# Where the last two expert groups of a mixture-of-experts layer are summed into the output

## The chip, the core and the metric

One core of a Trainium2 chip runs the whole layer in one launch. The metric is device time in microseconds (us) of one execution. TensorE (PE) multiplies, VectorE (DVE) and ScalarE (ACT) move and transform, GpSimd (POOL) helps, and the SyncE queue (SP) issues nearly all transfers.

## The reference

A decoder layer on 256 tokens of width 1024, float32: norm, one input projection, two kinds of attention, an output projection with a residual, and then a mixture of experts. The change touches only the end of the last part:

```python
g = jnp.argmax(g_logits, axis=-1)                 # 1 of 4 groups for each token
top_v, top_e = lax.top_k(e_logits, 2)             # 2 of the 8 experts in it
weight = p_group * jax.nn.softmax(top_v, axis=-1)
def run(args):                                    # for each expert e on its tokens
    xc = t[toks]
    hid = jax.nn.silu(xc @ w_gate[e]) * (xc @ w_up[e])
    return hid @ w_down[e]
y = jnp.zeros((N, D), t.dtype).at[slot_tok].add((out * slot_w[:, None]).astype(t.dtype))
x = x + hier_moe(...)                             # the residual
```

There are 32 experts; gate and up are 1024 x 256, down is 256 x 1024, so each matrix is 1 MB and the experts' weights are 96 MB.

## The kernel before

The kernel goes through the experts in order, as steps e = 0 to 31, and works on them in eight groups of four (G = 4, not the reference's groups). Each expert has 32 slots for tokens (CAP), so that a group fills 128 partitions.

- `prep(g)`, in the last step of the group before, builds with `places` a 0/1 matrix of slots (tiles Pm and Ps) and gathers the group's tokens by 32 PE passes (L615) into the tile xe.
- In step e, `gate` and `up` multiply the tokens of expert e by its two matrices (16 PE passes each, since a float32 product of the program is two passes in the trace; L658); `folded` transposes the result of expert e-1 (L675) and makes hT on DVE and ACT; `down` multiplies hT of expert e-2 by its down matrix (L693) and moves the product out of PSUM into the group's tile oG (L707 on ACT and L709 on DVE, four pieces).
- `weighted(st)` scales the slot matrix by the tokens' weights W, transposes it on PE (L642) and keeps it as pT. `combine(st)`, two steps into the next group, adds pT times oG of the whole group into the output sums y, which stay in four PSUM banks (L728, full 128 rows).
- The last group goes another way: `weighted_last` makes four repeated matrices, one for each expert (L628 on DVE, L630 on PE, L631 on ACT), into a tile oL; `moved` takes a down product out of PSUM in two pieces (L712, L713); and `spread` adds one expert's product into y with four 32-row tiles of PE (L718). `residual` adds the residual, which POOL copied to the tile res (L906), by a product with the identity (L733).
- `last` does the down product of expert 31, and the copies of y to res (L750, L752) and from there to the output (L753), in two halves.

PE keeps its program order (`pe`). Weights come through a ring of 16 one-megabyte tiles and seven more slots (`fill`, `unit`); SP issues each load as soon as the tile's last reader is done and an earlier load has landed. After step 28's down product stands `overflow`, a branch on whether an expert has more than 32 tokens; all engines pass it, and the body was not run here.

Of the kernel before, what the change touches and what calls it, by code (L numbers as in the profile page):

```python
# [9 lines left out]
F32 = mybir.dt.float32  # L10
# [4 lines left out]
AF = mybir.ActivationFunctionType  # L15
# [5 lines left out]
P = 128  # L21
# [30 lines left out]
def hybrid_layer_kernel(ctx: ExitStack, tc: tile.TileContext, x, xt, w_in, w_out, w_gate, w_up, w_down, smalls, relb, out):  # L52
# [534 lines left out]
    u = 16  # L587
    G = 4
    x2n = x2q.rearrange("t c k p -> t c p k")
    CROSS = [(j, c) for c in range(NC) for j in range(4)]  # L590
    g2p = A_COLS["g2p"][0]

    def places(g, c):
# [23 lines left out]
            gathered(st, q4, pg, 0, P)  # L617
        return st

    def weighted_last(st):  # L620
        t = pools["late"].tile([P, 2048], F32, name="oL", tag="late")
        st["o"], st["pT"] = t[:, :D].rearrange("p (i n) -> p i n", i=G), t[:, D:].rearrange("p (i t) -> p i t", i=G)
        for i in range(G):
            pt = ps.tile([P, 512], F32, name="ptr", tag="tr")
            for c in range(NC):
                q = st["P"][c][1].rearrange("p (j s) -> p j s", j=G)
                e = st["g"] * G + i
                nc.vector.tensor_scalar(q, st["P"][c][0][:, i : i + 1, :].broadcast_to([P, G, CAP]),  # L628
                                        W[:, c, e : e + 1], None, op0=ALU.mult)
                pe(nc.tensor.transpose(pt[:, c * P : (c + 1) * P], q.rearrange("p j s -> p (j s)"), ident))  # L630
            nc.scalar.activation(st["pT"][:, i, :], pt[:, :S], AF.Copy)  # L631

    def weighted(st):
        g = st["g"]
        if g == E // G - 1:
            return weighted_last(st)
# [59 lines left out]
    def down(e, st, hT, low):  # L696
        i = e % G
        dv = unit(place[e][2], low).rearrange("p (c n) -> p c n", c=2)
        pd = ps.tile([P, 512], F32, name="pd", tag="tr")
        down_product(hT, dv, pd, range(2), range(4))  # L700
        if st["g"] == E // G - 1:
            moved(st, i, pd, slice(0, P))
            return
        for j in range(4):
            dst = st["o"][i * CAP : (i + 1) * CAP, j * 256 : (j + 1) * 256]
            if j % 2 == 0:
                nc.scalar.activation(dst, pd[j * 32 : (j + 1) * 32, :256], AF.Copy)  # L707
            else:
                nc.vector.tensor_copy(dst, pd[j * 32 : (j + 1) * 32, :256])  # L709

    def moved(st, i, pd, rows):
        nc.scalar.activation(st["o"][rows, i, :P], pd[rows, :P], AF.Copy)  # L712
        nc.vector.tensor_copy(st["o"][rows, i, P:], pd[rows, P:256])  # L713

    def spread(st, i, pairs):
        for j, c in pairs:
            r = slice(j * CAP, (j + 1) * CAP)
            pe(nc.tensor.matmul(y[j][:, c * 256 : c * 256 + 256], st["pT"][r, i, c * P : (c + 1) * P],  # L718
                                st["o"][r, i, :], start=False, stop=i == G - 1 and c == NC - 1, tile_position=(j * CAP, 0)))

    y = []

# [13 lines left out]
    def last(e, st, hT, res):  # L736
        dv = unit(place[e][2]).rearrange("p (c n) -> p c n", c=2)
        pd = ps.tile([P, 512], F32, name="pd", tag="tr")
        down_product(hT, dv, pd, (0,), range(4))
        warmed(2, "pp")  # L740
        for nh in range(2):
            down_product(hT, dv, pd, (1,), (2 * nh, 2 * nh + 1))
            moved(st, G - 1, pd, slice(nh * 64, nh * 64 + 64))
            j0 = 2 * nh
            spread(st, G - 1, [(j, c) for c in range(NC) for j in (j0, j0 + 1)])
            for c, eng in enumerate((nc.scalar, nc.sync)):
                for j in (j0, j0 + 1):
                    dst = res[:, c, j * 256 : (j + 1) * 256]
                    if j == j0:
                        nc.scalar.activation(dst, y[j][:, c * 256 : c * 256 + 256], AF.Copy)  # L750
                    else:
                        nc.vector.tensor_copy(dst, y[j][:, c * 256 : c * 256 + 256])  # L752
# [127 lines left out]
    before, queue = None, []  # L880
    for e in range(1, E):
        g, i = divmod(e, G)
        old, old_t = st, t
        if i == 0:
            before, st = old, nxt
        t = gate(e, st)
        queue.append((e - 1, old, folded(old_t)))
        if i == 2 and g > 0:
            combine(before)
        up(e, st, t)  # L890
        if i == G - 1 and g < E // G - 1:
            nxt = prep(g + 1)
        if i == 2:
            weighted(st)
        if e == E - 1:
            hT = folded(t)
        if e > 1:
            down(*queue.pop(0), place[e][0])
        if e == OVER_E:
            overflow()  # L900
        if e == E - 1:
            rt_ = ring.tile([P, 2048], F32, name="res", tag="ring")
            res = rt_.rearrange("p (c n) -> p c n", c=NC)
# [4 lines left out]
    spread(st, 0, CROSS)  # L908
    spread(st, 1, CROSS)
    down(*queue.pop(0), place[E - 1][0])  # L910
    residual(0, res)
    residual(1, res)
    spread(st, 2, CROSS)
    last(E - 1, st, hT, res)


_OUTS = [((1, 256, 1024), "float32")]
# [71 lines left out]
```

## Time and profile before

| | |
|---|---|
| median of 3 runs | 344.23 us (343.37 to 344.47) |
| the profiled execution's own time | 344.96 us |
| its span | 343.2 us |
| busy PE, DVE, ACT, POOL | 314.5, 194.3, 139.9, 17.3 us |
| transfers | 123.20 MB, mean 359 GB/s |

The span runs from the first to the last recorded event; the execution's own time has 1.76 us more around it. Busy times are sums over stages with different limits, so the prediction reads stretches and single waits. Times such as 322.10 are us from the start of the span.

### The profile page before, as it was taken

The numbers are of one execution on the slowest core, as the hardware profiler recorded it, in microseconds if no ns is written. First come the engines' busy times: TensorE is split into PE (matmuls) and PEld (weight loads), VectorE is DVE, ScalarE is ACT, GpSimd is POOL, SyncE is SP. The second block draws the span as 40 slices with busy tenths as digits, with TensorE's granted clock in tenths as the row PEclk, the third lists the DMA queues.
The fourth block names the chain that finished last, engine by engine and source line by source line (L and its number), as shares of the span: only waits on it lengthen the run. The fifth ranks groups of instructions, "written<-read, shape, count | busy, mean of one in ns | idle before, by whom it ended". The sixth has DMA issues, their size and how long they took to land. (4 is left out here: it accounts for less than half of the span.)

```text
span 343.2 us, 7327 instructions
## 1 busy us (share of the span) xinstructions
PE 314.5 (92%) x2801; PEld 217.4 (63%) x2801; DVE 194.3 (57%) x599; ACT 139.9 (41%) x364; POOL 17.3 (5%) x25
## 2 busy tenths in 40 slices
PE   6999999999999999999999999998489669968893
PEld 2758877788777797576666766566257326625461
DVE  1867858869998658665463654736224522532502
ACT  4876667968886443423232232321112211211302
POOL 1100001000110140000000000000000000040000
PEclk9899999999999999999999999999989978989997
DMA  6999999999635888899999999999999999999903
GB/s 197 403 385 317 389 387 402 413 411 409 209 99 210 319 355 320 303 423 418 416 416 415 415 421 418 413 421 413 416 418 416 418 415 420 416 411 420 362 10 122
DMA packets 29496, 123.20 MB, mean 359 GB/s; under 512 B 2295, under 2 KB 3364, under 8 KB 21268
## 3 DMA queue, kind: packets, MB, share of 16 engines
q1 hardware_dynamic: 28868, 121.17, 89.1%
q0 software_dynamic: 304, 1.02, 1.0%
q8 instruction: 23, 0.38, 0.4%
q10 hardware_dynamic: 288, 0.52, 0.4%
q14 instruction: 13, 0.11, 0.1%
HBM read 121.64 MB, written 1.07 MB: 358 GB/s over the span
## 5 line engine op out<-in xcount | busy, mean ns | idle before, releaser
L658 PE MATMUL pgu<-u,xe 128*32 128x256 f32 x976 | 67.4, 395 | 10.1 <-ACT oG L707 4.8
L254 PE MATMUL pp<-hi,xh 128*128 128x512 f32 (+1 forms) x132 | 53.3, 405 | 2.6 <-ACT hi L243 2.6
L254 PE MATMUL pp<-lo,xh 128*128 128x512 f32 (+1 forms) x132 | 52.1, 399 | 0.3 <-POOL lo L244 0.2
L254 PE MATMUL pp<-hi,xl 128*128 128x512 f32 (+1 forms) x132 | 51.9, 393 | 0.0
L707 ACT ACTIVATE oG<-pd 32x256 f32<-32x256 f32 x56 | 21.0, 374 | 75.0 <-PE pd L693 61.4
L658 PEld LDWEIGHTS pgu<-u,xe 128*32 128x32 f32 x976 | 29.5, 111 | 34.6 <-ACT oG L707 8.6
L244 DVE TENSOR_TENSOR lo<-u,hi 128x512 fp32r<-128x512 f32 x62 | 43.1, 714 | 13.0 <-ACT hi L243 12.7
L243 ACT ACTIVATE hi<-u 128x512 fp32r<-128x512 f32 x64 | 38.9, 626 | 18.3 <-PE pp L254 12.6
L709 DVE COPY oG<-pd 32x256 f32<-32x256 f32 x56 | 23.7, 423 | 38.7 <-ACT oG L707 36.8
L693 PE MATMUL pd<-u,hT 128*32 128x256 f32 x496 | 34.9, 394 | 6.6 <-DMA u<-in_w_down_dram 6.6
L254 PEld LDWEIGHTS pp<-hi,xh 128*128 128x128 f32 x132 | 25.1, 190 | 9.6 <-ACT hi L243 4.0
L254 PEld LDWEIGHTS pp<-lo,xh 128*128 128x128 f32 x132 | 25.3, 192 | 7.4 <-issue 1.0
L254 PEld LDWEIGHTS pp<-hi,xl 128*128 128x128 f32 x132 | 25.2, 191 | 4.6
L670 DVE COPY u<-pgu 128x256 f32<-128x256 f32 x30 | 12.7, 422 | 26.7 <-PE pgu L658 23.6
L615 PEld LDWEIGHTS pg<-Ps,x2q 128*128 128x128 f32 x224 | 25.5, 192 | 2.9 <-DVE gu L678 2.9
L693 PEld LDWEIGHTS pd<-u,hT 128*32 128x32 f32 x496 | 14.5, 112 | 20.0 <-DVE u L670 7.5
L615 PE MATMUL pg<-Ps,x2q 128*128 128x128 f32 x224 | 26.9, 278 | 0.0
L728 PE MATMUL y<-oG,pT 128*128 128x256 f32 x112 | 26.4, 391 | 0.0
L728 PEld LDWEIGHTS y<-oG,pT 128*128 128x128 f32 x112 | 21.8, 200 | 2.8
L678 DVE TENSOR_REDUCE gu<-ptr 128x64 f32<-128x256 f32 x32 | 13.6, 425 | 14.5 <-PE ptr L675 13.8
L675 PEld LDWEIGHTS ptr<-sm,u 128*128 128x128 f32 x120 | 13.4, 147 | 13.1 <-issue 9.9
L675 PE MATMUL ptr<-sm,u 128*128 128x128 f32 x120 | 21.0, 301 | 0.0
(166 smaller groups left out, 342.0 us busy)
## 6 DMA issues: line engine op xcount, KB each, us to landing
u<-in_w_up_dram SPq DMA_DIRECT2D x31, 1024.0 KB, 19.9
u<-in_w_gate_dram SPq DMA_DIRECT2D x30, 1024.0 KB, 19.9
u<-in_w_down_dram SPq DMA_DIRECT2D x30, 1024.0 KB, 19.9
u<-in_w_in_dram SPq DMA_DIRECT2D x11, 1024.0 KB, 12.0
u<-in_w_out_dram SPq DMA_DIRECT2D x4, 1024.0 KB, 14.6
x<-in_w_gate_dram SPq DMA_DIRECT2D x2, 1024.0 KB, 9.0
u<-in_w_in_dram SPq DMA_DIRECT2D x2, 512.0 KB, 6.0
x<-in_x_dram SPq DMA_DIRECT2D x2, 512.0 KB, 10.9
```

What stands on the lines that cost most here:

```text
L243: nc.scalar.activation(hi, raw, AF.Copy)
L244: (nc.gpsimd if u * 4 + k in (0,3,) else nc.vector).tensor_tensor(lo, raw, hi.bitcast(F32), op=ALU.subtract)
L254: yield lambda a=a, w=w, kk=kk, i=i: nc.tensor.matmul(pp, a, w[:, cols], start=first and kk == 0 and i == 0, stop=last and kk == len(hls) ...
L615: pe(nc.tensor.matmul(pg[:, j * P : (j + 1) * P], x2q[:, c, q4 * 4 + j, :], st["P"][c][1], start=c == 0, stop=c == NC - 1))
L658: pe(nc.tensor.matmul(pg[q * CAP : (q + 1) * CAP, :HID], st["xe"][:, k, j0 : j0 + CAP], wv[:, k, :], start=r == 0, stop=r == KC // ROWS_Q ...
L670: nc.vector.tensor_copy(t[:, HID : 2 * HID], pg[:, :HID])
L675: pe(nc.tensor.transpose(pt[:, j * P : (j + 1) * P], t[:, j * P : (j + 1) * P], ident))
L678: nc.vector.tensor_reduce(gu[:, :2], parts[:, :2], axis=AX.X, op=ALU.add)
L693: pe(nc.tensor.matmul(pd[j * 32 : (j + 1) * 32, :256], hT[:, c, :], dv[:, c, j * 256 : (j + 1) * 256], start=c == 0, stop=c == 1, tile_pos ...
L707: nc.scalar.activation(dst, pd[j * 32 : (j + 1) * 32, :256], AF.Copy)
L709: nc.vector.tensor_copy(dst, pd[j * 32 : (j + 1) * 32, :256])
L728: pe(nc.tensor.matmul(y[j][:, c * 256 : c * 256 + 256], st["pT"][:, c * P : (c + 1) * P], st["o"][:, j * 256 : (j + 1) * 256], start=st["g ...
```

## The change

It treats the last two groups (6 and 7, steps 24 to 31; APART = 6) as the last one was treated before. Their four repeated transposes are split off as `repeated` (DVE) and `weighted_last` (PE, ACT), one a step in steps 24 to 27, and two a step in steps 28 and 29. `spread` of expert e stands in the step after its `down`, for all of experts 24 to 28; `combine` of group 6 goes. The residual's first half stands at the end of step 30 and its second ahead of the down product of expert 30. The tiles oL (two of them) and res come from the ring. `last` does the last down product and the last `spread` whole, and then all copies, four on ACT and four on DVE. The core of the diff:

```diff
+    def spare(name):
+        used["ring"].append(len(units))
+        return ring.tile([P, 2048], F32, name=name, tag="ring")
+    def repeated(st, i):
+        e = st["g"] * G + i
+        for c in range(NC):
+            q = st["P"][c][1].rearrange("p (j s) -> p j s", j=G)
+            nc.vector.tensor_scalar(q, st["P"][c][0][:, i : i + 1, :].broadcast_to([P, G, CAP]),
+                                    W[:, c, e : e + 1], None, op0=ALU.mult)
+    def weighted_last(st, i):
+        pt = ps.tile([P, 512], F32, name="ptr", tag="tr")
+        for c in range(NC):
+            pe(nc.tensor.transpose(pt[:, c * P : (c + 1) * P], st["P"][c][1], ident))
+        nc.scalar.activation(st["pT"][:, i, :], pt[:, :S], AF.Copy)
...
-        if st["g"] == E // G - 1:
-            moved(st, i, pd, slice(0, P))
+        if st["g"] >= APART:
+            moved(st, i, pd)
...
+    def last(st, hT, dv, pd, res):
         for nh in range(2):
             down_product(hT, dv, pd, (1,), (2 * nh, 2 * nh + 1))
+        moved(st, G - 1, pd)
+        spread(st, G - 1)
+        for c in range(NC):
+            for j in range(4):
+                dst = res[:, c, j * 256 : (j + 1) * 256]
+                if j < 2:
+                    nc.scalar.activation(dst, y[j][:, c * 256 : c * 256 + 256], AF.Copy)
+                else:
+                    nc.vector.tensor_copy(dst, y[j][:, c * 256 : c * 256 + 256])
+            for nh, eng in enumerate((nc.scalar, nc.sync)):
                 eng.dma_start(out[c * P : (c + 1) * P, nh * 512 : nh * 512 + 512], res[:, c, nh * 512 : nh * 512 + 512])
...
         if i == 0:
             before, st = old, nxt
+            if g >= APART:
+                last_group(st)
         t = gate(e, st)
         queue.append((e - 1, old, folded(old_t)))
-        if i == 2 and g > 0:
+        apart = () if g < APART else (i,) if g == APART else ((0, 1), (2, 3), (), ())[i]
+        if apart:
+            repeated(st, apart[0])
+        if i == 2 and 0 < g <= APART:
             combine(before)
         up(e, st, t)
+        for k, j in enumerate(apart):
+            if k:
+                repeated(st, j)
+            weighted_last(st, j)
         if i == G - 1 and g < E // G - 1:
             nxt = prep(g + 1)
-        if i == 2:
+        if i == 2 and g < APART:
             weighted(st)
+        if done:
+            spread(*done.pop())
...
+            if st2["g"] >= APART:
+                done.append((st2, e2 % G))
...
+        if e == E - 2:
+            residual(0, res)
+    residual(1, res)
     down(*queue.pop(0), place[E - 1][0])
-    residual(0, res)
-    residual(1, res)
-    spread(st, 2, CROSS)
-    last(E - 1, st, hT, res)
+    spread(*done.pop())
+    dv = unit(place[E - 1][2]).rearrange("p (c n) -> p c n", c=2)
+    pd = ps.tile([P, 512], F32, name="pd", tag="tr")
+    down_product(hT, dv, pd, (0,), range(4))
+    spread(st, 2)
+    warmed(2, "pp")
+    last(st, hT, dv, pd, res)
```

PE's order from the up product of expert 30 (weights u_3102) to the down product of expert 30, before. Here u_3177 and u_3278 are the down weights of experts 28 and 29, x_64 and u_3224 the gate and up weights of expert 31, u_3280 the down weights of expert 30:

```order
L658 MATMUL pgu<-u_3102,xe 32x256 x8
L630 MATMUL ptr<-sm,Ps 128x128 x8
L693 MATMUL pd<-u_3177,hT 32x256 x8
L658 MATMUL pgu<-x_64,xe 32x256 x8
L675 MATMUL ptr<-sm,u_3100 128x128 x4
L658 MATMUL pgu<-u_3224,xe 32x256 x8
L675 MATMUL ptr<-sm,x_64 128x128 x4
L693 MATMUL pd<-u_3278,hT 32x256 x8
L718 MATMUL y<-oL 128x256 x16
L693 MATMUL pd<-u_3280,hT 32x256 x8
L733 MATMUL y<-res,sm 128x256 x8
L718 MATMUL y<-oL 128x256 x8
```

The same place of PE now; the weights have other numbers (u_3180, u_3291, u_3293, u_3295), the lines have moved by six:

```order
L664 MATMUL pgu<-u_3102,xe 32x256 x8
L724 MATMUL y<-oL 128x256 x8
L699 MATMUL pd<-u_3180,hT 32x256 x8
L739 MATMUL y<-res,sm 128x256 x4
L664 MATMUL pgu<-x_64,xe 32x256 x8
L681 MATMUL ptr<-sm,u_3100 128x128 x4
L664 MATMUL pgu<-u_3291,xe 32x256 x8
L724 MATMUL y<-oL 128x256 x8
L681 MATMUL ptr<-sm,x_64 128x128 x4
L699 MATMUL pd<-u_3293,hT 32x256 x8
L739 MATMUL y<-res,sm 128x256 x4
L699 MATMUL pd<-u_3295,hT 32x256 x8
```

The eight transposes are gone from here, the spreads of experts 27 and 28 and both halves of the residual have come in ahead of the down product of expert 30, and a spread stands between expert 31's up product and its transposes.

The end of PE's order before, from the first half of the down product of expert 31 (u_3282):

```order
L693 MATMUL pd<-u_3282,hT 32x256 x4
L688 LDWEIGHTS zeros
L688 MATMUL warm<-zeros 128x512
L688 LDWEIGHTS zeros
L688 MATMUL warm<-zeros 128x512
L693 MATMUL pd<-u_3282,hT 32x256 x2
L718 MATMUL y<-oL 128x256 x4
L693 MATMUL pd<-u_3282,hT 32x256 x2
L718 MATMUL y<-oL 128x256 x4
```

And now, from the down product of expert 30:

```order
L699 MATMUL pd<-u_3295,hT 32x256 x8
L724 MATMUL y<-oL 128x256 x8
L699 MATMUL pd<-u_3345,hT 32x256 x4
L724 MATMUL y<-oL 128x256 x8
L694 LDWEIGHTS zeros
L694 MATMUL warm<-zeros 128x512
L694 LDWEIGHTS zeros
L694 MATMUL warm<-zeros 128x512
L699 MATMUL pd<-u_3345,hT 32x256 x4
L724 MATMUL y<-oL 128x256 x8
```

Two half spreads behind two quarter products have become one whole spread behind one half product; ahead of it stand the spreads of experts 29 and 30.

DVE's order in step 27 before, from the copy of the up product of expert 26 (u_2855) on; L599 writes the slot matrices Ps of group 7, u_2934 is expert 27's:

```order
L670 COPY u_2855<-pgu 128x256
L599 TENSOR_SCALAR Ps<-Pm,rstd 128x128 x2
L709 COPY oG<-pd 32x256 x2
L678 TENSOR_REDUCE gu<-ptr 128x64
L680 TENSOR_REDUCE gu<-ptr 128x64
L682 TENSOR_TENSOR hT<-gu 128x64
L670 COPY u_2934<-pgu 128x256
```

And now, with L632 for the repeated matrix of expert 27 and L719 for the new way out of PSUM:

```order
L676 COPY u_2855<-pgu 128x256
L632 TENSOR_SCALAR Ps<-Pm,W 128x128 x2
L597 TENSOR_TENSOR Pm<-R_1577,sm 128x128 x2
L719 COPY oL<-pd 128x128
L684 TENSOR_REDUCE gu<-ptr 128x64
L686 TENSOR_REDUCE gu<-ptr 128x64
L688 TENSOR_TENSOR hT<-gu 128x64
L676 COPY u_2934<-pgu 128x256
L599 TENSOR_SCALAR Ps<-Pm,rstd 128x128 x2
```

The two writes of Ps for group 7 have moved from ahead of step 27's work to behind the copy of expert 27's up product, since the transposes of expert 27 read those tiles till then.

## Rows read from the trace of the kernel before

**Rows 1.** The first line of the page.

```profile
span 343.2 us, 7327 instructions
```

**Rows 2.** Stretches: length, busy PE, PEld, DVE, ACT, POOL, granted clock, DMA share, GB/s.

```profile
280.00:290.00 10.00, 9.45 (x74) 6.11 (x74) 2.64 (x8) 1.77 (x5) 0.00 (x0) 0.75 1.02 416
305.00:310.00 5.00, 4.67 (x48) 1.86 (x38) 1.47 (x4) 0.88 (x3) 3.62 (x4) 0.66 1.02 413
328.00:335.00 7.00, 6.49 (x50) 4.09 (x46) 0.45 (x2) 0.55 (x2) 0.00 (x0) 1.00 0.00 0
```

**Rows 3.** SP's issue of the up weights of expert 31, in the timeline.

```profile
300.77 0.33 SPq L138 DMA_DIRECT2D u<-in_w_up_dram  x1
```

**Rows 4.** The page's list of loads: these, with the median time to landing last.

```profile
u<-in_w_up_dram SPq DMA_DIRECT2D x31, 1024.0 KB, 19.9
```

**Rows 5.** SP's longest wait of 280 to 310 us: total, times, longest.

```profile
SPq L138 <- DMA u<-in_w_gate_dram: 8.4, 4, 2.1
```

**Rows 6.** Timeline, steps 27 to 30: start, length, engine, line, tiles, passes, idle before and releaser.

```profile
292.68 3.84 PE L615 MATMUL pg<-Ps,x2q 128*128 128x128 f32 x32
...
293.15 0.42 DVE L670 COPY u<-pgu 128x256 f32<-128x256 f32 x1
...
300.89 1.07 PE L693 MATMUL pd<-u,hT 128*32 128x256 f32 x16 [0.93 <-DMA u<-in_w_down_dram]
...
303.28 0.43 DVE L709 COPY oG<-pd 32x256 f32<-32x256 f32 x1 [0.44 <-ACT oG L707]
...
304.42 1.07 PE L658 MATMUL pgu<-u,xe 128*32 128x256 f32 x16 [2.46 <-DVEq L758]
...
310.86 1.07 PE L658 MATMUL pgu<-u,xe 128*32 128x256 f32 x16 [1.17 <-DMA u<-in_w_gate_dram]
...
312.36 3.62 PE L728 MATMUL y<-oG,pT 128*128 128x256 f32 x16
...
316.91 0.44 PE L630 MATMUL ptr<-sm,Ps 128*128 128x128 f32 x2
...
319.65 1.07 PE L693 MATMUL pd<-u,hT 128*32 128x256 f32 x16
```

**Rows 7.** Timeline, step 31 to the end, same columns.

```profile
321.10 0.29 DVE L713 COPY oL<-pd 128x128 f32<-128x128 f32 x1 [1.76 <-ACT oL L712]
...
321.52 0.66 PE L675 MATMUL ptr<-sm,u 128*128 128x128 f32 x4
...
322.10 1.07 PE L658 MATMUL pgu<-u,xe 128*32 128x256 f32 x16
...
325.09 2.01 PE L718 MATMUL y<-oL 32*128 32x256 f32 x32
...
327.03 1.07 PE L693 MATMUL pd<-u,hT 128*32 128x256 f32 x16
...
328.03 3.72 PE L733 MATMUL y<-res,sm 128*128 128x256 f32 x16
...
331.68 1.15 PE L718 MATMUL y<-oL 32*128 32x256 f32 x16
...
332.76 0.64 PE L693 MATMUL pd<-u,hT 128*32 128x256 f32 x8
...
333.87 0.62 PE L693 MATMUL pd<-u,hT 128*32 128x256 f32 x4
...
335.18 1.13 PE L718 MATMUL y<-oL 32*128 32x256 f32 x8 [0.69 <-DVE oL L713]
...
337.74 1.13 PE L718 MATMUL y<-oL 32*128 32x256 f32 x8 [0.87 <-DVE oL L713]
...
338.94 0.76 DVE L752 COPY res<-y 128x256 f32<-128x256 f32 x2 [1.26 <-PE y L718]
```

**Rows 8.** Output rate, 330 to 343.2 us in 40 bins of 0.33 us.

```profile
GB/s 0 0 0 0 0 0 0 0 0 0 0 0 0 0 0 0 0 0 0 0 0 0 0 43 385 385 379 360 37 0 0 292 410 360 391 137 0 0 0 0
```

More of the change, by code (lines that the diff above doesn't have):

```diff
@@ L589, in hybrid_layer_kernel @@
     x2n = x2q.rearrange("t c k p -> t c p k")
-    CROSS = [(j, c) for c in range(NC) for j in range(4)]
+    APART = E // G - 2
     g2p = A_COLS["g2p"][0]
@@ L618, in prep, with last_group @@
         return st
-    def weighted_last(st):
-        t = pools["late"].tile([P, 2048], F32, name="oL", tag="late")
-        st["o"], st["pT"] = t[:, :D].rearrange("p (i n) -> p i n", i=G), t[:, D:].rearrange("p (i t) -> p i t", i=G)
[L623 to L631, printed above, removed]
+    def spare(name):
+        used["ring"].append(len(units))
+        return ring.tile([P, 2048], F32, name=name, tag="ring")
+    def last_group(st):
+        t = spare("oL")
+        st["o"], st["pT"] = t[:, :D].rearrange("p (i n) -> p i n", i=G), t[:, D:].rearrange("p (i t) -> p i t", i=G)
+    def repeated(st, i):
[9 more added lines that the diff above has]
+        nc.scalar.activation(st["pT"][:, i, :], pt[:, :S], AF.Copy)
     def weighted(st):
         g = st["g"]
-        if g == E // G - 1:
-            return weighted_last(st)
         pt = ps.tile([P, 512], F32, name="ptr", tag="tr")
@@ L709, in down, with moved, spread @@
                 nc.vector.tensor_copy(dst, pd[j * 32 : (j + 1) * 32, :256])
[L711 to L716, printed above, removed]
+    def moved(st, i, pd):
+        nc.scalar.activation(st["o"][:, i, :P], pd[:, :P], AF.Copy)
+        nc.vector.tensor_copy(st["o"][:, i, P:], pd[:, P:256])
+    def spread(st, i):
+        for c, j in [(c, j) for c in range(NC) for j in range(4)]:
             r = slice(j * CAP, (j + 1) * CAP)
             pe(nc.tensor.matmul(y[j][:, c * 256 : c * 256 + 256], st["pT"][r, i, c * P : (c + 1) * P],
-                                st["o"][r, i, :], start=False, stop=i == G - 1 and c == NC - 1, tile_position=(j * CAP, 0)))
+                                st["o"][r, i, :], start=False, stop=st["g"] == E // G - 1 and i == G - 1 and c == NC - 1, tile_position=(j * CAP, 0)))
     y = []
@@ L734, in residual @@
                                 start=False, stop=False))
[L736 to L740, printed above, removed]
+    def last(st, hT, dv, pd, res):
         for nh in range(2):
             down_product(hT, dv, pd, (1,), (2 * nh, 2 * nh + 1))
[L743 to L752, printed above, removed]
+        moved(st, G - 1, pd)
[8 more added lines that the diff above has]
+            for nh, eng in enumerate((nc.scalar, nc.sync)):
                 eng.dma_start(out[c * P : (c + 1) * P, nh * 512 : nh * 512 + 512], res[:, c, nh * 512 : nh * 512 + 512])
@@ L879, in hybrid_layer_kernel @@
         nc.vector.tensor_copy(flag, cm)
-    before, queue = None, []
+    before, queue, done = None, [], []
     for e in range(1, E):
@@ L897, in hybrid_layer_kernel @@
         if e > 1:
-            down(*queue.pop(0), place[e][0])
+            e2, st2, hT2 = queue.pop(0)
+            down(e2, st2, hT2, place[e][0])
+            if st2["g"] >= APART:
+                done.append((st2, e2 % G))
         if e == OVER_E:
             overflow()
-        if e == E - 1:
-            rt_ = ring.tile([P, 2048], F32, name="res", tag="ring")
-            res = rt_.rearrange("p (c n) -> p c n", c=NC)
+            res = spare("res").rearrange("p (c n) -> p c n", c=NC)
             for c in range(NC):
@@ L907, in hybrid_layer_kernel @@
                                           x2n[:, c, nh * 64 : (nh + 1) * 64, :])
-    spread(st, 0, CROSS)
-    spread(st, 1, CROSS)
+        if e == E - 2:
+            residual(0, res)
+    residual(1, res)
     down(*queue.pop(0), place[E - 1][0])
-    residual(0, res)
-    residual(1, res)
-    spread(st, 2, CROSS)
-    last(E - 1, st, hT, res)
+    spread(*done.pop())
[5 more added lines that the diff above has]
+    last(st, hT, dv, pd, res)
 _OUTS = [((1, 256, 1024), "float32")]
```

## The prediction

> **What bounds the kernel now.** I read the span first [rows 1], then stretches near the end, then SP's queue, then the timeline of PE. In the stretches the transfers are full (share 1.02, some 415 GB/s) up to 310, and from 328 to 335 there are none, while PE is busy for 6.49 of 7.00 us [rows 2]. So the weights set the pace until PE falls behind them, and the last 15 us belong to PE and what hangs on it. SP shows that no load waits for a free tile: what it waits for are earlier loads, up to 2.1 us at a time [rows 5]. The load of expert 31's up weights (SP's sixth load from the last: after it come the down weights of experts 29, 30 and, in three pieces, 31) is issued at 300.77 [rows 3] and lands about 19.9 us later [rows 4], at 320.7. In the timeline PE takes these weights at 322.10, right behind the transposes of 321.52 and with no wait for a transfer [rows 7]; its last such wait ended at 310.86 [rows 6]. From there on PE is late, by 1.4 us at this point.
>
> **The data's chain after the change.** Nothing in the change touches a load, so expert 31's up weights still land at 320.7; I take 320.9 as PE's earliest start. What then stands in PE's order up to the last spread, each from start to start:
> - up product of 31: 1.00, as the down product of 327.03 to 328.03, which has as many passes of the same size [rows 7];
> - three spreads (28, 29, 30), each alone: 1.08 (331.68 to 332.76), together 3.24 [rows 7];
> - transposes of expert 31: 0.58 (321.52 to 322.10) [rows 7];
> - down products of 29 and 30: 1.00 each [rows 7];
> - half the residual: 3.65 (328.03 to 331.68) / 2 = 1.83 [rows 7];
> - first half of the last down product and the two warming products: 1.11 (332.76 to 333.87) [rows 7];
> - second half, its way out of PSUM, and the start of the last spread: 1.31 for a quarter (333.87 to 335.18) [rows 7], and 0.05 for twice the passes, an estimate (x8 and x4 differ by 0.02 in length).
>
> The sum is 11.12, so the last spread starts at 332.0, where it started at 337.74 [rows 7]: 5.7 us earlier. The residual and two spreads that stood behind the last transfers are what went.
>
> **The output's end.** DVE's first copy started 1.20 after the spread (338.94 against 337.74) and a copy takes 0.38 [rows 7]. Now it has four, not two: the third ends 2.34 after the spread, at 334.3, and the fourth at 334.7. I count on no earlier start, though the spread now has twice the passes in about the same length (1.15 against 1.13) [rows 7]. Before, the output left in two bursts, 337.6 to 339.5 and 340.2 to 341.9, each half of 1.05 MB at some 385 GB/s [rows 8]; the second began some 0.9 after DVE's copy of 338.94 had ended (339.32). Now nearly all leaves in one burst of 1.05 MB / 385 GB/s = 2.7 us, from 334.3 + 0.9 = 335.2 to 337.9. The 1.3 from the last byte to the end of the span (341.9 to 343.2) stay. End of span: **339.2**, 4.0 us less. The burst eats about 1 us of what the chain gains, and two more copies 0.8.
>
> A rule of the Trainium skill bears on the burst (Trainium Kernel Development and Optimization, Key Constraints): transfers issued from SP, ACT and GpSimd all run on the same 16 DMA engines, and more issuing engines only save issue time. By that rule one burst is twice as long, as in my sum; if two queues added up, it would be 1.4 us shorter. The trace leans to the rule: both old bursts already came from two queues.
>
> **Is PE ready at 320.9?** It was at 322.10. Between step 27 and there, in us:
> - Step 27: the transposes for expert 27 and the late Ps of group 7. The gather's 32 passes started at 292.68; DVE's copy of the up product ended at 293.57 [rows 6], and Ps comes behind it now. With 0.3 for Ps (estimate) the gather starts at 293.9: +1.2. What waits behind it is all of PE. The three pairs of transposes of steps 24 to 26 I price at nothing: in 24 and 25 PE waits for weights (1.45 ahead of 278.33, in 25), and in 26 a pair stood there before. Without that cover each is 0.44 [rows 6].
> - Four spreads (24 to 27) at 1.08: +4.3 [rows 7]. The combine of group 6 goes: -3.6 [rows 6].
> - Four pairs of transposes in step 30, 2.74 (316.91 to 319.65) [rows 6], move to 28 and 29, where two of four waits for DVE fall under other work: -0.2.
> - Half the residual: +1.8 [rows 7]. POOL's copies for it run from the branch on, some 10 us ahead, and cost nothing.
> - Two waits for weights, 0.93 and 1.17 [rows 6], are eaten up: -2.1.
> - The branch of step 28: PE waited until DVE was through. DVE ended 303.28 + 0.43, 2.8 after the down product began (300.89); with two pieces in place of four it is 1.7 (321.39 - 319.65) [rows 6, 7]: -1.1. This lies between 0 and -1.1.
> - Step 29 ran at half clock (0.66 over 305 to 310) [rows 2]: 5.27 (304.42 to the end of work at 309.69) [rows 6] for four groups that take 3.6 at full clock (1.00, 0.58, 1.00, 1.00) [rows 7]. The low clock came behind two waits of PE, 0.93 and 2.46, which I expect to be shorter: -1.7. This lies between 0 and -1.7, and at half clock the step's new work would cost 0.9 more.
>
> Together -1.4: PE is ready at 320.7, just as the weights land. So data and PE meet, and what PE loses ahead of this point costs nearly its full length.
>
> The profiled execution took 344.96 for its 343.2 of span, the runs' median is 0.73 below it: 339.2 + 1.76 - 0.73 = **340.2**. A measurement here can tell about 0.3% (1 us) from no change.
>
> **Rivals.**
> 1. *PE comes late because its clock drops in steps 28 and 29 as before.* For it: low stretches followed waits of PE in this trace (0.75 over 280 to 290, 0.66 over 305 to 310) [rows 2], and one wait stays at the branch. Against: PE has more work and less waiting around it. Price 1.7 to 2.6: 341.9 to 342.8, still faster.
> 2. *Changing between PE's tile shapes costs more than the lone spread shows.* Two spreads side by side took 1.94 (325.09 to 327.03), one alone 1.08 [rows 7], so a change is worth some 0.22, and it is in my price once. Four spreads and half a residual ahead of 320.9 bring ten changes, 2.2 if each came on top: 342.3. The Trainium skill has the rule (TensorEngine Tiling (Array Packing), Key Properties): a change of tiling mode, not of tile alone, drains TensorE. By the rule such changes are paid; the trace agrees with a cost, but its start-to-start times hold it already.
> 3. *Better than that*: the copies start after five of the spread's eight products and the burst is less of a lump, or PE's price in the last chain is lower. At most the burst's 1.4 and 0.3 of copies: 338.5.
> 4. *Slower: the loads come late.* oL twice and res now take three of the ring's 16 tiles from step 24 on, so the last loads go into tiles that other readers free. Place: SP's queue; price: us for us at the end, and slower from 4.0 us of delay on (345.2 for 5). Against: the new predecessors are read in steps 24 to 26, over by 292.68 [rows 6], and SP came to the first of these loads at 300.77 [rows 3]: 8 us of room.
> 5. *Nothing comes of it*: several of PE's losses at once, near 344. Data and PE meeting so closely leaves this open.
>
> **Chances.** Forecast 0.58 (339.3 to 341.4), rival 1 0.19, rival 2 0.06, rival 3 0.08, rival 4 0.04, rival 5 0.05. Rivals 1 and 2 are on the faster side nearly whole, so faster 0.88, same 0.07, slower 0.05. The range that leaves out 2 in 10 runs from rival 3's 338.5 to rival 1's 342.8.
>
> **What the profile would show.** Right: loads end by 328 as before; expert 31's up product starts near 321 and the last spread near 332; four copies each on ACT and DVE; one output burst of nearly 3 us; no combine in step 30; gate 29 within 2 us of the end of down 26. Wrong: SP's up load of expert 31 after 301; full-clock rows missing from steps 28 to 31; PE waiting for POOL at the residual, or for DVE at the gather for more than 1.5.

## The result, and the profile after

The changed kernel takes 339.52 us (339.01 to 340.49, 4 runs) where the kernel before took 343.80 (343.14 to 344.47, 4 runs) beside it: a ratio of 0.9879, 95% interval 0.9854 to 0.9904. It is faster by 4.3 us, or 1.2%; the forecast was 340.2, in a range of 338.5 to 342.8. The profiled execution took 340.49.

The first line of the page of the changed kernel answers to [rows 1]:

```profile
span 338.7 us, 7426 instructions
```

The stretches of [rows 2], of the changed kernel (length, busy PE, PEld, DVE, ACT, POOL, granted clock, DMA share, GB/s):

```profile
280.00:290.00 10.00, 9.47 (x90) 5.92 (x90) 3.74 (x13) 2.06 (x6) 0.00 (x0) 0.94 1.02 415
...
305.00:310.00 5.00, 3.54 (x44) 1.84 (x44) 2.83 (x6) 1.02 (x3) 4.16 (x4) 1.00 1.01 411
...
328.00:335.00 7.00, 3.77 (x50) 1.72 (x42) 1.71 (x5) 1.49 (x5) 0.00 (x0) 1.00 0.09 33
```

The granted clock is 0.94 for 0.75 and 1.00 for 0.66; only the second turns out to be the change's (see PE's readiness below). From 328 on PE works 3.77 us where it worked 6.49, and the first part of the output falls into the stretch.

The timeline of the changed kernel, steps 27 to 31, answers to [rows 3] and [rows 6] (start, length, engine, line, tiles, passes, idle before and releaser):

```profile
290.08 1.07 PE L664 MATMUL pgu<-u,xe 128*32 128x256 f32 x16 [0.55 <-DMA u<-in_w_up_dram]
...
291.89 3.84 PE L615 MATMUL pg<-Ps,x2q 128*128 128x128 f32 x32 [0.37 <-DVE Ps L599]
...
300.13 0.33 SPq L138 DMA_DIRECT2D u<-in_w_up_dram  x1
...
300.19 0.44 PE L638 MATMUL ptr<-sm,Ps 128*128 128x128 f32 x2
...
301.45 1.15 PE L724 MATMUL y<-oL 32*128 32x256 f32 x16
...
304.96 1.07 PE L664 MATMUL pgu<-u,xe 128*32 128x256 f32 x16 [1.36 <-DVEq L760]
305.15 4.16 POOL L920 COPY res<-x2q 128x512 f32<-128x512 f32 x4 [175.04 <-DMA u<-in_w_up_dram]
...
307.51 0.88 DVE L688 TENSOR_TENSOR hT<-gu 128x64 f32<-128x64 f32 x1
307.55 0.44 PE L638 MATMUL ptr<-sm,Ps 128*128 128x128 f32 x2
...
308.65 0.94 DVE L632 TENSOR_SCALAR Ps<-Pm,W 128x128 f32<-128x128 f32 x2
...
309.45 0.52 PE L638 MATMUL ptr<-sm,Ps 128*128 128x128 f32 x2 [1.46 <-DVE Ps L632]
309.90 1.15 PE L724 MATMUL y<-oL 32*128 32x256 f32 x16
...
320.14 1.07 PE L664 MATMUL pgu<-u,xe 128*32 128x256 f32 x16
```

Expert 31's up weights are issued at 300.13 (0.64 earlier than in the other profile; the offset is there long before step 24, 0.13 at 122 us and 0.5 more by 161 us, so it is not the change's), and land 19.9 later by its list of loads, at 320.03; PE takes them at 320.14, and the profile lists no wait of PE for a load behind 304.96. Counted from this issue, the span ends after 38.57 us, and after 42.43 in the kernel before: 3.9 us of the gain lie behind it. Where PE does wait for this load in the runs below, it starts some 0.1 behind the landing, so data and PE do meet. The row of that list (this load, KB, us to landing):

```profile
u<-in_w_up_dram SPq DMA_DIRECT2D x1, 1024.0 KB, 19.9
```

Gate 29 waits 1.36 and not 2.46, as forecast. Not forecast is the wait of 1.46 for DVE in step 29; in the same place stand POOL's copies for the residual.

The end of the changed kernel's timeline, for [rows 7]:

```profile
323.80 1.99 PE L739 MATMUL y<-res,sm 128*128 128x256 f32 x8
...
325.73 1.07 PE L699 MATMUL pd<-u,hT 128*32 128x256 f32 x16
...
329.45 0.60 PE L694 MATMUL warm<-zeros 128*128 128x512 bf16 x2
329.99 0.64 PE L699 MATMUL pd<-u,hT 128*32 128x256 f32 x8
...
331.35 1.15 PE L724 MATMUL y<-oL 32*128 32x256 f32 x16 [0.72 <-DVE oL L719]
332.57 1.21 ACT L751 ACTIVATE res<-y 128x256 f32<-128x256 f32 x4 [1.60 <-PE y L724]
332.67 1.42 DVE L753 COPY res<-y 128x256 f32<-128x256 f32 x4 [1.37 <-PE y L724]
```

and the output, for [rows 8] (328 to 338.7 us, 40 bins of 0.27 us):

```profile
GB/s 23 23 8 0 0 0 0 0 0 0 0 0 0 0 0 0 0 0 0 0 0 0 0 8 367 390 375 368 398 368 383 368 414 375 107 0 0 0 0 0
```

From the start of expert 31's up product to the last spread it is 11.21 us, from there to the end 7.35; the forecast had 11.12 and 7.2. There is one burst, from about 334.4 to 337.2, where there were two.

### The profile page after: what moved, and what is told of

Its sections match the earlier page's. It is cut to its first block, busy times and chain, and to the rows that moved or that the text cites. A ratio compares the mean times of both kernels' runs of the same rounds, so it can differ in the third digit from the quotient of the medians.

```text
span 338.7 us, 7426 instructions
## 1 busy us (share of the span) xinstructions
PE 311.8 (92%) x2855; PEld 215.2 (64%) x2855; DVE 193.7 (57%) x600; ACT 138.6 (41%) x362; POOL 17.4 (5%) x25
## 3 DMA queue, kind: packets, MB, share of 16 engines
HBM read 121.64 MB, written 1.07 MB: 362 GB/s over the span
## 5 line engine op out<-in xcount | busy, mean ns | idle before, releaser
L664 PE MATMUL pgu<-u,xe 128*32 128x256 f32 x976 | 65.9, 388 | 8.4 <-ACT oG L713 4.2
L713 ACT ACTIVATE oG<-pd 32x256 f32<-32x256 f32 x48 | 17.9, 374 | 60.9 <-PE pd L699 49.2
L715 DVE COPY oG<-pd 32x256 f32<-32x256 f32 x48 | 20.3, 423 | 31.7 <-ACT oG L713 30.0
L699 PE MATMUL pd<-u,hT 128*32 128x256 f32 x496 | 34.0, 391 | 4.4 <-DMA u<-in_w_down_dram 3.5
L734 PE MATMUL y<-oG,pT 128*128 128x256 f32 x96 | 22.3, 387 | 0.0
L681 PE MATMUL ptr<-sm,u 128*128 128x128 f32 x120 | 20.1, 291 | 0.0
L734 PEld LDWEIGHTS y<-oG,pT 128*128 128x128 f32 x96 | 18.3, 196 | 2.3
## 6 DMA issues: line engine op xcount, KB each, us to landing
u<-in_w_up_dram SPq DMA_DIRECT2D x31, 1024.0 KB, 19.9
u<-in_w_gate_dram SPq DMA_DIRECT2D x30, 1024.0 KB, 19.9
u<-in_w_down_dram SPq DMA_DIRECT2D x30, 1024.0 KB, 19.9
```

What stands on the lines that cost most here:

```text
L664: pe(nc.tensor.matmul(pg[q * CAP : (q + 1) * CAP, :HID], st["xe"][:, k, j0 : j0 + CAP], wv[:, k, :], start=r == 0, stop=r == KC // ROWS_Q ...
L681: pe(nc.tensor.transpose(pt[:, j * P : (j + 1) * P], t[:, j * P : (j + 1) * P], ident))
L699: pe(nc.tensor.matmul(pd[j * 32 : (j + 1) * 32, :256], hT[:, c, :], dv[:, c, j * 256 : (j + 1) * 256], start=c == 0, stop=c == 1, tile_pos ...
```

## The experiments

Two theories stood against each other. **A**, that of the prediction: the end is set by a chain from the point at which PE takes expert 31's up weights, which is where their landing and PE's readiness meet; the gain is work that left this chain or was put into gaps ahead of its loads. **B**: the gain is PE's regained clock and its shorter waits in steps 25 to 29, wherever the work stands. The lag from PE's start on expert 31's up weights to the end of the span ("the last chain") is a measure that doesn't move with what lies upstream, though it does with the loads that land later. Where PE comes to this product late, the lag from the landing counts. Every lag is read from one execution. Every ratio is against the kernel before on the same chip; the changed kernel was measured again on the chip of the residual put back, the halves and group 6 whole, and not on the two chips of the other runs.

**The changed kernel again**, as the base for the others, with no edit.

> The changed kernel once more, on the chip of the next three, so that they can be set against it. Both theories: 4.0 to 4.5 us under the kernel before, and the up product of expert 31 starts within 0.3 us of its weights' landing (19.9 us after SP's issue of them).

340.48 us, ratio 0.9912 (0.9887 to 0.9937); span 338.3, last chain 319.81 to 338.3, 18.49 (18.56 in the profile above). Single executions spread by some 3 us (339.45 to 342.52), so differences under 0.5 us are read from profiles here and not from medians. The gain on this chip is 3.5 us (the kernel before took 344.01), less than the 4.0 to 4.5 expected; PE starts on the weights 0.1 behind their landing, as expected.

**Both halves of the residual behind the down product of expert 30**, where they were:

```diff
-        if e == E - 2:
-            residual(0, res)
-    residual(1, res)
     down(*queue.pop(0), place[E - 1][0])
+    residual(0, res)
+    residual(1, res)
```

> The changed kernel with both halves of the residual behind the down product of expert 30 again, as before. Theory A (the gain is the PE work that no longer stands behind the last transfers): the half that had moved ahead of expert 31's up product comes back into the last chain and PE has to wait for those weights, so the end comes 1.8 us later than in the changed kernel. Theory B (the gain comes from the clock and the waits of steps 25 to 29, where PE has more work and stays at full clock): no difference beyond 0.4 us, since nothing changes there.

343.62 us, ratio 0.9986 (0.9970 to 1.0003): nothing of the gain is left that the measurement can tell, where 1.8 us of loss were expected. Its timeline, step 31:

```profile
316.92 1.07 PE L664 MATMUL pgu<-x,xe 128*32 128x256 f32 x16 [1.23 <-SPq L760]
...
319.40 1.07 PE L664 MATMUL pgu<-u,xe 128*32 128x256 f32 x16 [0.83 <-SPq L760]
...
324.47 1.07 PE L699 MATMUL pd<-u,hT 128*32 128x256 f32 x16 [1.33 <-DMA u<-in_w_down_dram]
325.47 3.72 PE L739 MATMUL y<-res,sm 128*128 128x256 f32 x16
```

PE now waits three times, 3.39 in all, and then does the residual's 3.65 behind the last of these waits. (SPq L760, SP's passage of the branch, is named as releaser of two of them although it was over long before; the second starts 0.1 behind the landing of its load.) The last chain is 21.7, so 3.2 longer. The missing 1.4 is the second half: in the changed kernel it stands in the gap ahead of expert 30's down weights, which I had not seen as a gap. The prediction's sum counted it as work in the chain that nothing else hides.

**The residual moved alone**, in the kernel before (the first half at the end of step 30, the second ahead of the spreads and the down product of expert 30; nothing else of the change. POOL's copies move behind the branch in the program, but ran there before too):

```diff
-        if e == E - 1:
+        if e == OVER_E:
             rt_ = ring.tile([P, 2048], F32, name="res", tag="ring")
...
+        if e == E - 2:
+            residual(0, res)
+    residual(1, res)
...
     down(*queue.pop(0), place[E - 1][0])
-    residual(0, res)
-    residual(1, res)
```

> The kernel before with one part of the change alone: the residual's first half at the end of step 30 and its second ahead of the spreads behind step 31. Theory A: PE is already 1.4 us late at expert 31's up weights and never waits from there on, so 3.65 us of its work moved forward only push what follows, and the time is that of the kernel before within 0.5 us. A theory in which the residual's place by itself is worth what its undoing cost (some 2.7 us): 2.5 us or more faster.

345.02 us, ratio 1.0013 (0.9992 to 1.0033): no gain. Its timeline:

```profile
323.16 1.07 PE L658 MATMUL pgu<-u,xe 128*32 128x256 f32 x16
```

The up weights of expert 31 landed at 319.65 in this run (19.9 behind their issue at 299.75); PE comes 3.5 later, without a wait. There was no gap for the residual to go into. So neither the move of the residual nor the rest of the change alone gains anything beyond the measurement, and both together gain 3.5 us: the rest makes gaps, the residual fills them.

**The last product, spread, copies and output in halves again**, as before the change:

```diff
-        moved(st, G - 1, pd)
-        spread(st, G - 1)
+            moved(st, G - 1, pd, slice(nh * 64, nh * 64 + 64))
+            spread(st, G - 1, (2 * nh, 2 * nh + 1))
+            for c, eng in enumerate((nc.scalar, nc.sync)):
...
```

> The changed kernel with the last down product, spread, copies and output in two halves, as before. Theory A: the second half spread starts 2.56 us after the first and the end comes 5.46 us behind it, 8.0 in all, against 7.35 from the single spread to the end now: 0.6 us later than the changed kernel. Rival: the single burst of 1 MB at the very end costs more than the halves' extra chain, and the halves are 0.5 to 1.0 us faster.

340.10 us, ratio 0.9889 (0.9876 to 0.9902). By the profile the last chain is 19.11 (319.19 to 338.3), 0.6 longer than in the run of the changed kernel beside it, as A has it; but the median is not longer. It is inconclusive: whether the end is done in halves or whole is worth less than the medians tell.

**Group 6 combined whole again**, only group 7 expert by expert:

```diff
-    APART = E // G - 2
+    APART = E // G - 1
-        apart = () if g < APART else (i,) if g == APART else ((0, 1), (2, 3), (), ())[i]
+        apart = () if g < APART else ((0, 1), (2, 3), (), ())[i]
```

> The changed kernel with group 6 combined as a whole in step 30 again (its four repeated transposes and spreads gone); group 7 as changed. Theory A: the combine's 3.6 us stand behind the landing of expert 30's gate weights, PE comes to expert 31's up weights about 1.4 us after they have landed instead of on time, and the end is 1.4 us later. Rival: what group 6 gained in step 30 it paid in steps 27 to 30 (four spreads of 1.08 and a late gather, 5.5 us against 3.6), and the time is the same or up to 0.7 us shorter.

340.87 us, ratio 0.9912 (0.9892 to 0.9931), no different from the changed kernel by the medians. Its timeline, steps 29 to 31:

```profile
302.58 1.94 PE L664 MATMUL pgu<-u,xe 128*32 128x256 f32 x16 [2.30 <-DVEq L760]
...
311.18 3.62 PE L734 MATMUL y<-oG,pT 128*128 128x256 f32 x16
...
320.11 1.07 PE L664 MATMUL pgu<-u,xe 128*32 128x256 f32 x16
```

This has what the prediction's first rival feared: the long wait at the branch and half clock in step 29 (1.94 a product, 1.07 at full clock), as before the change. The weights, issued at 299.08, landed 20.2 later at 319.28, and PE takes them at 320.11, so it is 0.7 late (0.1 lies between landing and start anyway). From the landing to the end it is 19.3, in the changed kernel 18.6 and 18.7: the long wait, the half clock and the whole combine, less the four spreads and the transposes that they stand in for, cost 0.7. That is the worth of treating group 6 expert by expert, by the profile: half of the 1.4 that A expected. It speaks against B, since wait and low clock are back and most of the gain stays.

**The clock alone**, in the kernel before: products with zeros in steps 24, 25 and 28, at places where PE would wait:

```diff
         up(e, st, t)
+        if e in (24, 25, 28):
+            warmed(3, "pp")
...
             down(*queue.pop(0), place[e][0])
+        if e in (24, 25, 28):
+            warmed(4, "pp")
```

> The kernel before, with products of zeros (seven in each of steps 24, 25 and 28) put where PE waits for weights or for the branch, so that its clock need not fall in step 29; nothing else is changed. Theory A (the gain is work taken from behind the last transfers): step 29 is shorter by up to 1.7 us, but PE then only waits longer for the gate weights of expert 30, and the time is that of the kernel before within 0.5 us. Theory B (the gain comes from the clock and the waits of steps 25 to 29): 1.5 us or more under the kernel before.

344.28 us, ratio 1.0014 (0.9987 to 1.0041). Executions differed more than elsewhere (342.67 to 347.98), and the profiled one (347.49) is one of the long ones. Its timeline, steps 29 and 30:

```profile
303.22 1.07 PE L658 MATMUL pgu<-u,xe 128*32 128x256 f32 x16 [1.48 <-DVEq L758]
...
307.20 1.07 PE L693 MATMUL pd<-u,hT 128*32 128x256 f32 x16 [1.32 <-DMA u<-in_w_down_dram]
...
309.68 1.93 PE L658 MATMUL pgu<-u,xe 128*32 128x256 f32 x16 [1.42 <-ACT oG L707]
...
312.45 5.27 PE L728 MATMUL y<-oG,pT 128*128 128x256 f32 x16
```

and the stretch behind:

```profile
310.00:315.00 5.00, 5.00 (x26) 3.38 (x19) 1.00 (x4) 0.64 (x2) 0.00 (x0) 0.50 1.02 422
```

Step 29 runs at full clock (1.07), and what it gains is given back at once: PE waits 1.32 for a load, and 1.42 ahead of gate 30. Behind these two waits the granted clock falls to 0.50, one step later than before, and the combine takes 5.27 for 3.62. B is out as the whole cause: it expected a gain of 1.5 us or more, and the median of 12 runs has none. That the gain is given back at these waits is shown for this long execution alone; where the shorter ones lose it is open.

**PE made late by 1 us**, four zero products ahead of expert 31's up product:

```diff
+        if e == E - 1:
+            warmed(4, "pp")
         up(e, st, t)
```

> The changed kernel with four products of zeros (0.27 us each, 1.1 in all) ahead of the up product of expert 31. Theory A: PE comes to weights and chain 1.0 us later and the end moves by the same 1.0 us, since the chain from there on has no slack. Theory B, or any in which the last transfers or the output set the end: less than 0.4 us.

341.02 us, ratio 0.9917 (0.9898 to 0.9937), against 340.48 and 0.9912 without, on another chip. Its timeline:

```profile
319.33 1.07 PE L664 MATMUL pgu<-u,xe 128*32 128x256 f32 x16
```

The weights, issued at 298.56, landed 20.0 later at 318.56; PE comes 0.77 after that, so 0.67 late, and the last chain is 18.57, no shorter. From landing to end it is 19.3, 0.7 more than where the two meet: from this point on lateness of PE costs its full length in this profile. The ratios, 0.0005 or 0.2 us apart, can't tell 0.7 from nothing.

**Without the two warming products** ahead of the last half product:

```diff
     spread(st, 2)
-    warmed(2, "pp")
     last(st, hT, dv, pd, res)
```

> The changed kernel without the two warming products ahead of the last half of the down product. Theory A: they stand in the chain, 0.54 us, and PE has been busy all along, so the clock stays full and the end comes 0.5 us earlier. Rival: the last down weights land only just ahead of these products (some 328.8 us), PE waits for them in their place and nothing is gained; or the clock falls, and 0.5 us or more are lost.

339.75 us, ratio 0.9883 (0.9858 to 0.9909). The last chain is 17.95, 0.54 less, what the pair takes in the chain (329.45 to 329.99). The last spread in its timeline:

```profile
330.53 1.15 PE L724 MATMUL y<-oL 32*128 32x256 f32 x16 [0.72 <-DVE oL L719]
```

The last spread still takes 1.15, so the clock holds without them. The 0.54 is the profile's; by their intervals the ratios of the two kernels do not differ.

**The residual's copies on ACT**, to keep POOL away from DVE:

```diff
-                    nc.gpsimd.tensor_copy(res[:, c, nh * 512 : (nh + 1) * 512].rearrange("t (p k) -> t p k", k=KC),
...
+                nc.scalar.activation(res[:, c, nh * 512 : (nh + 1) * 512].rearrange("t (p k) -> t p k", k=KC),
```

> The changed kernel with the copies of the residual on ACT, not on POOL. In the changed kernel PE waited 1.46 us in step 29 for DVE, whose small operations took up to three times their length while POOL copied. Theory A: that wait falls to 0.4 and PE is earlier by 1 us in step 29, but expert 31's up weights land no earlier, so the wait goes there and the time stays the same within 0.4 us. Rival C (POOL's copies cost what they cost PE): 1 us faster.

341.75 us, ratio 0.9937 (0.9914 to 0.9960): no gain, and whether it is slower than with POOL is open (0.9912, up to 0.9937, for the changed kernel again). Its timeline, step 29:

```profile
303.45 3.15 ACT L921 ACTIVATE res<-x2q 128x512 f32<-128x512 f32 x3 [1.01 <-DVEq L760]
...
308.00 0.23 DVE L688 TENSOR_TENSOR hT<-gu 128x64 f32<-128x64 f32 x1 [1.39 <-ACT gu L685]
308.15 0.48 DVE L632 TENSOR_SCALAR Ps<-Pm,W 128x128 f32<-128x128 f32 x2
...
308.48 0.52 PE L638 MATMUL ptr<-sm,Ps 128*128 128x128 f32 x2 [1.99 <-DVE Ps L632]
```

The edit did not do what it was for: all four copies ran in step 29, three of them ahead of all of ACT's own work there and the fourth (306.78) ahead of the step of ACT that DVE needs; DVE waited for ACT 1.39, and PE for DVE 1.99 and not the 0.4 expected. It does show the one thing in question, though: with POOL idle the two DVE operations take 0.23 and 0.48, where they took 0.88 and 0.94.

**POOL's copies held back** until the last of the four repeated matrices (pT) is there, by two tiny copies of it ahead of them:

```diff
             res = spare("res").rearrange("p (c n) -> p c n", c=NC)
+        if e == E - 3:
+            for a in (0, 512):
+                nc.gpsimd.tensor_copy(res[:, :, a : a + 1], st["pT"][:, 3, 0:2].unsqueeze(2))
```

> The changed kernel with POOL's copies of the residual held back, by small copies of the tile pT of expert 27 into their targets, until the repeated transposes of step 29 are through. Theory A: PE's wait for DVE in step 29 falls from 1.46 to 0.4 us, which shows that POOL's copies had slowed DVE; PE then waits about 1 us longer for expert 31's up weights, and the time is the same within 0.4 us. Rival C: 1 us faster.

340.35 us, ratio 0.9885 (0.9851 to 0.9918). PE's waits in 300 to 322 us of its trace (total, times, longest):

```profile
PE pgu L664 <- DVEq L760: 1.4, 1, 1.4
PE ptr L638 <- DVE Ps L632: 0.7, 2, 0.4
PE pd L699 <- SPq L760: 0.6, 1, 0.6
PE pgu L664 <- SPq L760: 0.4, 1, 0.4
PE pgu L664 <- DMA u<-in_w_up_dram: 0.2, 1, 0.2
```

The wait of 1.46 is 0.37 here, so it was POOL's doing. But the microsecond comes back as waits for loads, 0.6, 0.4 and 0.2 in this stretch. In the changed kernel the same stretch has 1.4 and 1.8 in the first two kinds and no other wait. So removing the contention makes PE early, and early is worth nothing. Another wait, 0.72 ahead of expert 30's down product (325.99), makes the last chain 19.29; these weights landed 21.4 behind their issue in this execution, and 19.9 in the changed kernel's.

**A version out of what was learnt**: no warming products, POOL's copies held back, the spread of expert 28 ahead of expert 31's up product, and the last copies in the order of the output's four pieces, each piece issued as soon as its two copies are there:

```diff
+        if e == E - 1:
+            spread(*done.pop())
...
-        for c in range(NC):
-            for j in range(4):
+        for nh in range(2):
+            for c, eng in enumerate((nc.scalar, nc.sync)):
+                for j in (2 * nh, 2 * nh + 1):
...
-    warmed(2, "pp")
```

> The changed kernel with four more edits that theory A prices: no warming products (0.54 us), POOL's copies later (PE 1 us earlier in step 29), the spread of expert 28 ahead of expert 31's up product, where PE then has that time (1.07 us out of the chain, less what the next down weights take back, some 0.5), and the last copies and outputs in the order of the output's halves (0.3 us). From the start of expert 31's up product to the end of the span 16.8 to 17.4 us, against 18.5 in the changed kernel, and 1.0 to 1.5 us under it. If the output burst or the last weights bind, 17.9 or more.

339.19 us, ratio 0.9854 (0.9822 to 0.9886), span 336.9, the lowest median here, 1.3 us under the changed kernel measured again on another chip (340.48); but the intervals of the changed kernel (0.9854 to 0.9904 in the result), of the one without warming products and of the one with POOL's copies held back overlap with it. Its timeline and output (326 to 337, bins of 0.28 us):

```profile
319.95 1.07 PE L664 MATMUL pgu<-u,xe 128*32 128x256 f32 x16
...
329.94 1.15 PE L724 MATMUL y<-oL 32*128 32x256 f32 x16 [0.72 <-DVE oL L719]
331.16 0.94 ACT L752 ACTIVATE res<-y 128x256 f32<-128x256 f32 x3 [1.60 <-PE y L724]
```

```profile
GB/s 30 15 7 7 7 0 0 0 0 0 0 0 0 0 0 0 0 0 0 0 0 0 0 7 365 387 358 395 380 395 380 365 387 365 30 0 0 0 0 0
```

The last chain is 16.95, within what was expected. From the last spread to the end it is 6.96 and not 7.35, since the burst starts about 1.4 after the first copy and not 1.85. But the weights landed at 319.14 (20.2 behind 298.94), and PE comes 0.8 after that, the spread of 318.87 being in the way. From landing to end it is 17.8, in the changed kernel 18.6 and 18.7: of the 1.6 that left the last chain some 0.9 is gain. That is the warming products (0.54) and the earlier burst (0.39). The spread set ahead gained next to nothing: its 1.08 left the chain, but PE comes 0.7 late, and the transposes behind the up product, which the spread no longer parts from it, wait for DVE and take 0.98 (320.95 to 321.93) and not 0.58.

## Why the prediction held, step by step

**The data's chain** held nearly row by row: up product 1.00, spreads 1.08, 1.08 and 1.08, transposes 0.58, down products 1.00; only half the residual takes 1.93 where 1.83 was counted. It gave 11.21 for 11.12. That the residual and two spreads left the end is confirmed for the residual by its return (343.62).

**The output's end** held: 7.35 for 7.2. From the last spread to the burst it is 3.07 (3.2 counted), the burst takes some 2.8 (2.7), and some 1.5 follow it (1.3). One burst through two issuing queues, at 367 to 414 GB/s, is no faster than the weights through SP's queue (415 GB/s over 280 to 290). The rule of the Trainium skill (Trainium Kernel Development and Optimization, Key Constraints), that transfers of all issuers share 16 DMA engines, agrees with this trace: had two queues added up, the burst would have been 1.4 us. That the old bursts came from two queues, the prediction's reason, decides nothing, since the new one does too.

**PE's readiness** came out right in the sum and wrong in three terms, so the agreement of the sum is luck; and a PE ready ahead of the landing would have shown the same start. To set both profiles beside each other I add the 0.64 of upstream offset to the times of after:

| | predicted | measured |
|---|---|---|
| up to PE's up product of step 27 (291.68 before, 290.08 after) | 0 | -0.96 |
| step 27, up product to gather | +1.2 | +0.81 |
| gather to expert 31's up product (29.42 before, 28.25 after) | -2.6 | -1.17 |
| sum | -1.4 | -1.3 |

The rows of the kernel before for this, and the stretch of step 26 in the kernel with the residual moved alone, whose steps 24 to 27 are those of the kernel before:

```profile
291.68 1.07 PE L658 MATMUL pgu<-u,xe 128*32 128x256 f32 x16
...
304.46 4.16 POOL L906 COPY res<-x2q 128x512 f32<-128x512 f32 x4 [174.22 <-DVEq L758]
```

```profile
280.00:290.00 10.00, 9.19 (x97) 5.78 (x92) 3.56 (x12) 2.41 (x7) 0.00 (x0) 1.00 1.02 417
```

The first line of the table is the clock in step 26: the stretch of 280 to 290 went from 0.75 to 0.94, and PE, late for expert 27's up weights before, now waits 0.55 for them. But that is not shown to be the change's: with the residual moved alone the stretch has 1.00 and PE waits 0.76 for these weights (289.75), with the same work on PE up to there. The profiled execution of the kernel before, from which the prediction set out, was the one with a low clock in step 26. In the second line, DVE was ready earlier than by my reading (the wait for Ps is 0.37).

The third line has the step that failed: "POOL's copies for it run from the branch on, some 10 us ahead, and cost nothing". They cost 1.1, by way of DVE. The copies themselves are not new: in the kernel before they ran in the same place (304.46, and 3.62 us of them over 305 to 310 in [rows 2]), and there DVE's product for hT grew only to 0.29. New is that the change puts DVE's repeated matrices, which PE waits for, into these 4.16 us. The two pairs of transposes in step 29 and the wait between them take 2.35 from start to the spread, where the two in step 28 take 1.26 (300.19 to 301.45). The rest of what this line misses is small: 0.1 for the longer half of the residual, and 0.13 between the transposes of 319.43 and the up product beyond their 0.58, where PE meets the landing. The other terms are there: the wait at the branch 1.1 shorter (2.46 to 1.36), step 29 at full clock (1.07 and 0.66), no wait for weights listed behind 304.96, no combine. The clock of step 29 does go with the kernel: over 305 to 310 it is 0.66, 0.64 and 0.62 in the three kernels in which PE waits 2.3 to 2.5 at the branch (the one before, the residual moved alone, group 6 whole), and 1.00 in the changed kernel, both times.

**That data and PE meet** was the centre, and held: PE starts 0.11 behind the landing. What the meeting means I had only half: making PE late costs its length (by the run with zero products ahead), and making it early gains nothing (by POOL's copies held back).

**The residual** was priced wrongly by its place: 1.8 for the half that leaves the chain. Its return costs 3.1 to 3.2, for both halves stand in gaps: one ahead of expert 31's weights, one ahead of expert 30's down weights.

**The rivals.** The first, clock and waits as before in steps 28 and 29, is in the run with group 6 whole, which costs 0.7 and not 1.7 to 2.6. That doesn't price the rival by itself, though: in this run PE is also spared four spreads and has a combine in their place. No run has the low clock and the change's full work together. The second, changes of tile shape at 0.2 more each, falls: spreads between other products take 1.07 or 1.08 throughout, as the lone one did [rows 7]. The Trainium skill's rule on such changes (TensorEngine Tiling (Array Packing), Key Properties) may be what the 0.1 between 1.08 and half of 1.94 is; nothing above that is seen. Loads that come late through the ring (the fourth) are not seen: but for a trickle (23 GB/s up to 328.7) they end by 328.

## What to carry to other kernels

Where transfers and an engine meet at one point, an edit's price depends on which of the two is late there: moving work ahead of the last loads pays only if there is a gap for it, and making gaps pays only if there is work to fill them; two edits that measure as nothing alone can be the whole gain together. So list every wait for a load behind the moved work's old place and in front of it, not only the last one. And work on an engine "off the path" has a price if it slows one that is on it: look at the longest of an operation's durations, not its mean. And what one execution shows of the clock can be that execution's: compare a second trace before a change is given credit for it.

## What the runs showed that I had not expected

DVE is slowed while POOL copies. Over the whole trace of the changed kernel, two lines of DVE (min, median and max in ns, first and last start):

```profile
L688 DVE TENSOR_TENSOR hT<-gu x32: 214/225/884, 141.7 to 324.0; 128x64 f32<-128x64 f32 x32
```

```profile
L632 DVE TENSOR_SCALAR Ps<-Pm,W x16: 273/279/740, 265.3 to 309.3; 128x128 f32<-128x128 f32 x16
```

and the second in the kernel with POOL's copies held back:

```profile
L632 DVE TENSOR_SCALAR Ps<-Pm,W x16: 275/279/286, 263.9 to 307.5; 128x128 f32<-128x128 f32 x16
```

The two long ones, 0.88 and 0.74 (nearly four and nearly three times the medians), fall into POOL's four copies of 1.04 each (4.16), and are gone without them; the first is 0.60 long where it meets the copies in the kernel with these held back (312.62). The Trainium skill has it (SBUF — State Buffer, Who interferes with whom): a DVE operation with two operands in SBUF, or a tensor_scalar in one of its two-port modes, contends with GpSimd for a shared port pair, and whichever comes second is blocked until the other is done. The trace agrees with the sizes (an operation grows by less than one copy's length), and with DVE's reductions from PSUM in the same copies, which keep their 0.41 to 0.42; in which mode the TENSOR_SCALAR ran it does not show.

In the one profiled execution of the kernel with zero products the granted clock's fall moved and did not go: full speed in step 29, then half speed (0.50) one step on, behind two new waits of PE. And the last products keep full clock without the two warming products.
